# HGRN2/Conformer decoder trunk on one core: where the sums of weight blocks are made, and the order of the first stages

## The chip, the cores and the metric

One core of one Trainium2 chip runs the whole program. The metric is the device time of that core in microseconds (us), the median of three runs. Engines are named as in the profile: PE (TensorE, matmuls), PEld (its weight loads), DVE (VectorE), ACT (ScalarE), POOL (GpSimd), SP (SyncE, which issues nearly all transfers). POOL issues the transfers that add into their destination.

## The reference

Two layers on a sequence of 1024 tokens of width 1024. Each has a token mixer, a squared-ReLU MLP of width 4096, and a layer norm behind each. The first mixer is a gated linear recurrence (8 heads of 128), the second a causal convolution module.

```python
mix = hgrn2_mixer(x, a_w_in[j], lb_all[j], a_norm_g[j], a_w_out[j])      # layer 0
    proj = h @ w_in                       # columns q | forget | value | gate
    f = lb32 + (1.0 - lb32) * sigmoid(fz); k = 1.0 - f
    o = chunkwise_gated_recurrence(silu(q), k, v, cumsum(log f))
    o = rms_norm(o) * norm_g * silu(g);   mix = o @ w_out
mix = conformer_conv_mixer(x, ...)                                        # layer 1
x = layer_norm(DEEPNORM_ALPHA * x + mix, ln_mix_g[i], ln_mix_b[i])
ff = jnp.square(jax.nn.relu(x @ ffn_w1[i])) @ ffn_w2[i]
x = layer_norm(DEEPNORM_ALPHA * x + ff, ln_ffn_g[i], ln_ffn_b[i])
```

## The kernel before

**Products.** Float32 matrices are cut into a high part (a cast to float32r, on ACT) and a low part (the difference, on DVE): `cut` (L412) and `Slots.split` (L70). A product is three matmuls per tile: high by high, high by low, low by high. Many products are also made by a seven-product scheme on 2 by 2 blocks. Its seven forms of the weights run in the order 1, 2, 6, 5, 7, 3, 4 (`ORDER`, L45). With the four blocks w0 to w3 they are: 1: w0; 2: w1; 6: w0+w2+w3; 5: w2+w3; 7: w0+w2; 3: w0+w1+w2+w3; 4: w3. So each group of four blocks needs its sums from somewhere.

**Stages in time.** (a) The values' stage, 0 to 98 us: the value projection in seven forms (`v_products`, L463), 48 matmuls each. (b) The pairs, 109 to about 490 us: twelve pairs of projection blocks (`PAIRS`, L37; a "q" pair makes query and forget gate of one head, a "g" pair the output gates of two heads), seven forms of 12 matmuls each. Between the groups of three matmuls lies a `slot` (L795), four to a form and 28 to a pair. From the second pair on, a slot advances the recurrence of a finished head by 240/308 of a step (`pace`). A recurrence of one head and one half of the tokens has 15 steps (`recurrence`, L603), two can be under way at a time, and the second starts when the first has made seven steps. (c) The output projection. (d) The first MLP up, about 520 to 900 us, in seven forms whose sums are made on DVE (class `Forms`); its results go to DRAM (`hf`). (e) The first MLP down, 900 to 1200 us. (f) The convolution module, to about 1600 us, the second MLP up behind it, and the second MLP down, about 1900 to 2243 us.

**Sums of the values and pairs.** `pair_sums` (L394) makes them in DRAM: two plain transfers on SP copy blocks, then transfers on POOL add the others in, each waiting for the one before it. They are due a number of ticks later (`later`, `tick`; a slot is one tick, a tile of the values' stage four). The sums for pairs 0 to 2 start in the values' stage, those of pair p+3 in pair p. `load_form` (L564) then loads one raw form of 256 KB, and `make_form` (L575) cuts it on ACT and DVE, some forms ahead of its product, into the ring `fs` of six slots. Two of these six lie at 136 and 140 KB, where the last outputs of the values' stage (`VO[4]`) wait for their store.

**Sums of the down MLPs.** Class `Blocks` (L162) makes them anew in both down stages. For forms 1 and 2 it loads two blocks (w0, w2 and w1, w3), adds them on DVE and stores the sum (`pair`). For 6, 5 and 3 it loads two operands and adds, for 7 it loads a stored sum, for 4 a block. Blocks and operands are 512 KB each, and a form of one block is 24 matmuls.

**Orders.** Up to L930 the queues of PE, POOL and SP hold instructions in the order in which they are written. DVE and ACT are ordered by the planner, which sorts by when it expects each input. Behind L930 the planner orders all queues. Each queue runs in order, so an instruction that waits holds all behind it. `spare` (L1227) loads weights of later stages ahead of time during the first MLP: DVE marks the moment, POOL copies a mark into the buffer `next`, SP loads into it. `residual` (L1285) gates the loads of the kept rows `y` in the same way with eight copies on POOL.

Of the kernel before, what the change touches and what calls it, by code (L numbers as in the profile page):

```python
# [8 lines left out]
F32 = mybir.dt.float32  # L9
# [6 lines left out]
P = 128  # L16
# [20 lines left out]
PAIRS = [("q", 0), ("q", 1), ("q", 2), ("g", 0), ("q", 3), ("q", 4), ("g", 1), ("q", 5), ("q", 6), ("g", 2), ("q", 7), ("g", 3)]  # L37
# [122 lines left out]


class Blocks(Slots):  # L162


    def __init__(self, blocks, *rest):
        super().__init__(*rest)
        self.blocks = blocks

    def load(self, pieces=1):

        (i, c), slot = self.todo.pop(0), self.slots()
        self.queue.append(slot)
        w, pair = self.blocks[c]
        srcs = {1: (w[0], w[2]), 2: (w[1], w[3]), 6: (pair[0], w[3]), 5: (w[2], w[3]), 7: (pair[0],), 3: (pair[0], pair[1]), 4: (w[3],)}[i]
        got = [self.raws() for _ in srcs]
        for raw, src in zip(got, srcs):
            self.nc.sync.dma_start(out=raw, in_=src)
        if i in (1, 2):
            self.split(slot, got[0])
            self.vector.tensor_tensor(out=got[1], in0=got[1], in1=got[0], op=ALU.add)  # L180
            self.nc.sync.dma_start(out=pair[i - 1], in_=got[1])
        else:
            if len(got) > 1:
                self.vector.tensor_tensor(out=got[0], in0=got[0], in1=got[1], op=ALU.add)
            self.split(slot, got[0])
        yield
        self.count(slot)
# [78 lines left out]
def body(ctx, tc, d, out):  # L266
# [127 lines left out]
    def pair_sums(t, w, gap, half=False):  # L394
        n = 1 if half else 2

        def flat(x):
            return x.rearrange("a p n -> p a n")

        nc.sync.dma_start(out=flat(t)[:, 0:2], in_=flat(w)[:, 0 : 4 : n] if n == 2 else flat(w)[:, 0:2])  # L400
        if n == 2:
            nc.sync.dma_start(out=flat(t)[:, 2:4], in_=flat(w)[:, 0:2])
        parts = [lambda: nc.gpsimd.dma_start(out=flat(t)[:, 0:2], in_=flat(w)[:, 2:4], accum_op=ALU.add)]
        for i in (2, 3) if n == 2 else (1,):
            parts.append(lambda i=i: nc.gpsimd.dma_start(out=flat(t)[:, i], in_=flat(t)[:, i - 1], accum_op=ALU.add, max_dma_last_dim=4096))
        parts.append(lambda: summed.append(t))
        for i, part in enumerate(parts):
            later((min(i, len(parts) - 2) + 1) * gap, part)

    summed = []  # L410
# [52 lines left out]
    def v_products(i):  # L463
        for t, parts in enumerate(v_form(i)):
            product(banks[:, 4 + t] if i in (2, 5, 3) else banks[:, t], parts, i in (1, 2, 5))
            v_out(i, t)
            if t == 3 and i in (2, 5, 6):
                p = {2: 0, 5: 1, 6: 2}[i]
                pair_sums(psum[p], d["wp"][p], 8)
            tick(4)  # L470

    for k in range(4):
# [17 lines left out]
    psum = [dram.tile([4, P, HT], F32, name=f"psum{p}") for p in range(12)]  # L490
    vsum = dram.tile([2, 2, P, 1024], F32, name="vsum")
    for j in range(2):
        pair_sums(vsum[:, j], d["wv"][:, j], 4, True)
# [9 lines left out]
    cut_x(2, x10)  # L503
    cut_v(2, a1)
    for t in range(NTB):
        v_out(1, t)

# [7 lines left out]

    for k in range(4):
        vector.tensor_tensor(out=x00[:, k], in0=x00[:, k], in1=x01[:, k], op=ALU.subtract)
        cut_x(5, x00, (k,))
    add_v(a2, a2, a3)
    cut_v(5, a2)  # L520
    v_products(2)

    for k in range(4):
        vector.scalar_tensor_tensor(out=t6[:, k], in0=x00[:, k], scalar=-1.0, in1=x11[:, k], op0=ALU.mult, op1=ALU.subtract)
        cut_x(6, t6, (k,))
    add_v(a0, a2, a0)
    cut_v(6, a0)
    outs_v(5)
    sum_v(s7, 0)
    sum_v(a1, 1)  # L530
    v_products(5)

    for k in range(4):
        vector.tensor_tensor(out=x01[:, k], in0=x11[:, k], in1=x01[:, k], op=ALU.subtract)
        cut_x(7, x01, (k,))
    cut_v(7, s7)
    for k in range(4):
        vector.scalar_tensor_tensor(out=x10[:, k], in0=t6[:, k], scalar=-1.0, in1=x10[:, k], op0=ALU.mult, op1=ALU.subtract)
    outs_v(6)
    v_products(6)  # L540

    cut_x(3, x11)
    cut_v(3, a1)
    outs_v(4)
    v_products(7)
    cut_x(4, x10)
# [3 lines left out]
    vector.tensor_tensor(out=sm[:, 0], in0=lg, in1=lg, op=ALU.subtract)  # L550
    nc.scalar.activation(sm[:, 1], sm[:, 0], AF.Exp)
    vector.reciprocal(sm[:, 2], sm[:, 1])
    vector.tensor_tensor(out=sm[:, 3], in0=sm[:, 1], in1=sm[:, 2], op=ALU.mult)
    vector.tensor_tensor(out=lb, in0=sm[:, 3], in1=sm[:, 3], op=ALU.subtract)
    vector.tensor_scalar(out=oml, in0=lb, scalar1=-1.0, scalar2=1.0, op0=ALU.mult, op1=ALU.add)
    vector.tensor_scalar(out=nrm, in0=par[:, NRM : NRM + H], scalar1=1.0 / QSCALE, scalar2=None, op0=ALU.mult)
# [7 lines left out]
    def load_form():  # L564
        n = forms[0]
        if n == 7 * len(PAIRS):
            return
# [1039 lines left out]
```

## Time and profile before

| | |
|---|---|
| runs | 2244.64, 2245.33, 2246.27 us (median 2245.33) |
| profiled execution | 2245.43 us, of which the span is 2243.3 us |
| granted clock, mean | 0.977 |
| busy share of the span | PE 95%, PEld 78%, DVE 68%, ACT 47%, POOL 17% |
| bytes moved | 542.21 MB, mean 242 GB/s |

How to read it. The page gives the busy time of each engine. The view of waits says how long an engine stood still and whose work it then went on with. The timeline lists the instructions of an engine in order of time: start, duration, engine, line, operation, tiles, shapes, count, and in brackets the idle time before it with the releaser. The table of stretches gives for each stretch its length, the busy time of each engine with its count of instructions, then the granted clock as a share of full speed, the share of the time that the 16 DMA engines were busy, and GB/s. The view of transfers gives count, size and the median time from issue to landing. L201 is the line of a helper through which most matmuls and vector instructions go, so the tiles tell them apart: `vw` and `xf` belong to the values' stage, `fs` to the pairs, `qk`, `kd`, `T` and `state` to the recurrences, `fw` to the MLP up, `dw`, `dr` (weights) and `dh` (activations) to the MLP down.

### The profile page before, as it was taken

How to read it: one execution, taken by the hardware profiler on the slowest of the kernel's cores; microseconds unless marked ns; L12 is line 12 of the kernel's file. 1: busy time of each engine (PE TensorE's matmuls, PEld its weight loads, DVE VectorE, ACT ScalarE, POOL GpSimd, SP SyncE). 2: the span in 40 equal slices, each digit the busy share in tenths (PEclk: the TensorE clock that was granted, in tenths of full speed). 3: DMA queues.
4: the chain of work that ended last, by engine and by line, in shares of the span. 5: the costliest groups of instructions: out<-in, count | busy, mean ns of one | idle time of the engine just before them, and what ended most of it. 6: DMA issues, size and time to landing. Idle time of an engine off the chain costs nothing.

```text
span 2243.3 us, 27717 instructions
## 1 busy us (share of the span) xinstructions
PE 2124.4 (95%) x10056; PEld 1749.5 (78%) x10056; DVE 1527.5 (68%) x2078; ACT 1044.3 (47%) x1623; POOL 378.0 (17%) x337
## 2 busy tenths in 40 slices
PE   8799998989999999898999879899999999999998
PEld 6678787868888888677887768688888888877887
DVE  7378676777776666567765779689837444578556
ACT  5345444542365555333444546738662443434333
POOL 1111111001000000100001549549501000000001
PEclk9999999999999999999999989999999999999999
DMA  9866655434358687899997955375455898999762
GB/s 299 233 153 168 173 159 150 126 125 160 114 175 293 235 282 264 328 394 411 374 345 267 363 183 191 115 282 186 160 189 195 294 341 303 398 342 344 240 213 103
DMA packets 191657, 542.21 MB, mean 242 GB/s; under 512 B 18720, under 2 KB 47648, under 8 KB 190496
## 3 DMA queue, kind: packets, MB, share of 16 engines
q1 hardware_dynamic: 185504, 524.71, 64.9%
q0 software_dynamic: 6016, 15.73, 4.4%
q8 instruction: 79, 1.29, 0.2%
q14 instruction: 58, 0.48, 0.1%
HBM read 394.09 MB, written 176.69 MB: 254 GB/s over the span
## 4 chain that ended last, share of the span: by engine, by line
PE 44%; DMA 5%; POOL 3%; DVE 3%; ACT 2%; issue 1%; SPq 0%; DVEq 0%; POOLq 0%; ACTq 0%
PE ps L201 44%; POOL cb L201 3%; DMA next<-in_w_dram 1%; DMA next<-in_wpw_dram 1%; DMA hf<-ht 1%; DMA dr<-in_w_dram 1%; DMA pair<-dr 1%; DVE ps L201 1%; DMA dh<-hf 0%; DVE spare L201 0%; ACT spare L1236 0%; DVE dr L201 0%; ACT prod L1378 0%; ACT dw L70 0%; DMA raw<-in_w_dram 0%
## 5 line engine op out<-in xcount | busy, mean ns | idle before, releaser
L201 PE MATMUL ps<-dw,dh 128*128 128x512 f32 x2688 | 622.8, 394 | 32.2 <-ACT dw L70 20.3
L201 PEld LDWEIGHTS ps<-dw,dh 128*128 128x128 f32 x2688 | 509.9, 190 | 144.2 <-ACT dw L70 22.4
L201 PE MATMUL ps<-x1f,fw 128*128 128x512 f32 x1344 | 308.7, 390 | 0.7 <-DVE fw L201 0.3
L201 PEld LDWEIGHTS ps<-x1f,fw 128*128 128x128 f32 x1344 | 251.2, 188 | 53.0 <-DVE fw L201 0.8
L201 PE MATMUL ps<-xf,fs 128*128 128x512 f32 x1008 | 274.5, 410 | 11.7 <-ACT t L764 11.7
L201 PE MATMUL ps<-xa,wa 128*128 128x512 f32 x1152 | 273.5, 396 | 10.3 <-DMA wa<-ready 9.5
L201 PEld LDWEIGHTS ps<-xa,wa 128*128 128x128 f32 x1152 | 216.9, 190 | 56.4 <-DMA wa<-ready 10.5
L201 POOL TENSOR_TENSOR cb<-cb,prod 128x512 f32<-128x512 f32 x176 | 236.1, 1349 | 35.9 <-ACT prod L1378 25.1
L201 PEld LDWEIGHTS ps<-xf,fs 128*128 128x128 f32 x1008 | 180.6, 192 | 44.4 <-ACT t L764 12.1
L201 DVE SCALAR_TENSOR_TENSOR ps<-u,par,ps 128x512 f32<-128x512 f32 x288 | 204.5, 751 | 13.4 <-ACT ps L1390 9.9
L70 ACT CAST dw<-dr 128x1024 fp32r<-128x1024 f32 x112 | 116.8, 1050 | 183.9 <-DVE dr L201 86.4
L70 ACT CAST dh<-dh 128x1024 fp32r<-128x1024 f32 x112 | 117.1, 1050 | 142.4 <-DMA dh<-hf 139.5
L201 DVE TENSOR_TENSOR dw<-dr,dw 128x1024 fp32r<-128x1024 f32 x112 | 135.9, 1222 | 61.1 <-ACT dw L70 60.6
L201 DVE TENSOR_TENSOR dh<-dh 128x1024 fp32r<-128x1024 f32 x112 | 136.2, 1222 | 57.9 <-ACT dh L70 57.1
L201 PE MATMUL ps<-xc,wa 128*128 128x512 f32 x768 | 174.2, 389 | 0.0
L201 PEld LDWEIGHTS ps<-xc,wa 128*128 128x128 f32 x768 | 144.1, 188 | 29.9
L501 POOL TENSOR_TENSOR mv<-mv,nhalf 128x1 f32<-128x1 f32 x32 | 46.5, 1454 | 713.7 <-DVE mv L201 713.5
L1378 ACT ACTIVATE prod<-u,par 128x512 f32<-128x512 f32 x176 | 126.0, 722 | 61.0 <-POOL cb L201 60.3
L201 DVE TENSOR_TENSOR wa<-raw,wa 128x1024 fp32r<-128x1024 f32 x55 | 71.4, 1299 | 81.7 <-ACT wa L70 81.5
L201 DVE TENSOR_TENSOR dr<-dr 128x1024 f32<-128x1024 f32 x80 | 97.3, 1221 | 40.7 <-DMA dr<-pair 19.8
L70 ACT CAST wa<-raw 128x1024 fp32r<-128x1024 f32 x55 | 57.8, 1050 | 127.8 <-PE ps L201 103.8
L1243 POOL COPY next<-ss 128x1 f32<-128x1 f32 x37 | 20.7, 561 | 538.8 <-DVE ss L1233 234.7
(189 smaller groups left out, 2790.9 us busy)
## 6 DMA issues: line engine op xcount, KB each, us to landing
dr<-in_w_dram SPq DMA_DIRECT2D x128, 512.0 KB, 7.1
wa<-ready SPq DMA_DIRECT2D x122, 512.0 KB, 4.5
dh<-hf SPq DMA_DIRECT2D x112, 512.0 KB, 6.0
ready<-spare SPq DMA_DIRECT2D x74, 512.0 KB, 5.3
dr<-pair SPq DMA_DIRECT2D x64, 512.0 KB, 6.3
raw<-in_w_dram SPq DMA_DIRECT2D x51, 512.0 KB, 4.5
raw<-in_w1q_dram SPq DMA_DIRECT2D x36, 512.0 KB, 4.0
hf<-ht SPq DMA_DIRECT2D x64, 256.0 KB, 5.0
```

The costliest lines, as they stand in the source:

```text
L70: self.nc.scalar.copy(out=slot[:, 0, c], in_=raw[:, c])
L201: return op(*args, **kw)
L501: nc.gpsimd.tensor_tensor(out=dst, in0=src, in1=nhalf[:, :n], op=ALU.pow)
L1243: nc.gpsimd.tensor_copy(out=raw[:, :1], in_=now)
L1378: nc.scalar.activation(tp, u[:, k : k + HT], AF.Copy, scale=tap(j, k))
```

## The change

1. **Pairs.** `pair_sums` for the pairs is gone. The four raw blocks of a pair are loaded (48 loads in place of 84) into five buffers, and `make_form` adds them on DVE: four additions of 128x512 per pair. The ring `fs` has its last two slots at 160 and 164 KB. `PAIRS` has another order. A recurrence that is alone, while others wait or if it is the very first, takes every second step that is given to it.
2. **Values' stage.** DVE and ACT are in written order too, to the end of this stage. Additions and cuts are written between the tiles of the product before the one that uses them, and the forms of the last products are made earlier. The values' own sums stay transfers (`value_sums`).
3. **Second matrices of both MLPs (`w2`).** The class `Blocks` is gone. Sixteen groups of four blocks are summed in DRAM ahead of time by `block_sums`: two plain copies of 1 MiB on SP, then on POOL one adding transfer of 1 MiB and two of 512 KB. Ten are started in the pairs' stage (every eighth form), four in the first MLP up (behind every second group of weights, held back by a transfer of two elements that waits for the last form of that group), two behind the convolution. The down stages load one finished form of 512 KB at a time, with the plain `Slots`.

```diff
-PAIRS = [("q", 0), ("q", 1), ("q", 2), ("g", 0), ("q", 3), ("q", 4), ("g", 1), ("q", 5), ("q", 6), ("g", 2), ("q", 7), ("g", 3)]
+PAIRS = [("q", 0), ("q", 1), ("q", 2), ("q", 3), ("g", 0), ("q", 4), ("q", 5), ("g", 1), ("q", 6), ("q", 7), ("g", 2), ("g", 3)]
-class Blocks(Slots):
...
+    def value_sums(t, w, gap):
...
+        nc.sync.dma_start(out=flat(t), in_=flat(w)[:, 0:2])
+        later(gap, lambda: nc.gpsimd.dma_start(out=flat(t), in_=flat(w)[:, 2:4], accum_op=ALU.add))
+        later(2 * gap, lambda: nc.gpsimd.dma_start(out=flat(t)[:, 1], in_=flat(t)[:, 0], accum_op=ALU.add, max_dma_last_dim=4096))
+    def block_sums(name, layer, c, after=None, gap=0):
+        t = sums[name, layer, c] = dram.tile([4, P, 1024], F32, name=f"sum_{name}{layer}{c}")
+        v, w = t.rearrange("a p n -> p a n"), d[name][layer, c].rearrange("a p n -> p a n")
+        if after is not None:
+            nc.sync.dma_start(out=t[0:4:2, 0, 0:1], in_=after)
+        nc.sync.dma_start(out=v[:, 0:2], in_=w[:, 0:4:2])
+        later(gap // 2, lambda: nc.sync.dma_start(out=v[:, 2:4], in_=w[:, 0:2]))
+        parts = [lambda: nc.gpsimd.dma_start(out=v[:, 0:2], in_=w[:, 2:4], accum_op=ALU.add)]
+        for i in (2, 3):
+            parts.append(lambda i=i: nc.gpsimd.dma_start(out=v[:, i], in_=v[:, i - 1], accum_op=ALU.add, max_dma_last_dim=4096))
         for i, part in enumerate(parts):
-            later((min(i, len(parts) - 2) + 1) * gap, part)
+            later((i + 1) * gap, part)
+    def form(name, layer, c, i):
+        w, t = d[name][layer, c], sums[name, layer, c]
+        return {1: w[0], 2: w[1], 6: t[2], 5: t[1], 7: t[0], 3: t[3], 4: w[3]}[i]
...
+    early_order.enter_context(tc.manual_schedule(engines={mybir.EngineType.DVE, mybir.EngineType.Activation}))
...
-    v_products(2)
+    v_products(2, [lambda: x6(0, 1), lambda: x6(2, 3), lambda: add_v(a0, a2, a0), lambda: cut_v(6, a0)])
     outs_v(5)
     sum_v(s7, 0)
     sum_v(a1, 1)
-    v_products(5)
+    v_products(5, [lambda: x4(0, 1), lambda: x4(2, 3), bounds])
+    outs_v(6)
+    v_products(6, [lambda: x7(0, 1), lambda: x7(2, 3), lambda: cut_v(7, s7)])
+    v_products(7, [lambda: cut_x(3, x11, (0, 1)), lambda: cut_x(3, x11, (2, 3)), lambda: cut_v(3, a1)])
+    outs_v(4)
...
+    def load_block():
+        p, b = divmod(at_block[0], 4)
+        if p < len(PAIRS) and free:
+            at_block[0] += 1
+            raw = blocks_of[p, b] = free.pop(0)
+            nc.sync.dma_start(out=raw, in_=d["wp"][p, b])
     def make_form():
...
+        if i == 6:
+            plus(total, b[0], b[3])
+            plus(b[1], b[1], total)
+        elif i == 5:
+            plus(b[2], b[2], b[3])
+        cut(hi, lo, total if i == 6 else b[{1: 0, 2: 1, 5: 2, 7: 0, 3: 1, 4: 3}[i]])
+        if i == 2:
+            plus(b[0], b[0], b[2])
+        made.append(s)
+        if i in (5, 7, 3, 4):
+            free.append(b[{5: 2, 7: 0, 3: 1, 4: 3}[i]])
+            load_block()
...
+        if len(active) == 1 and (recs or active[0][0] == (0, 0)):
+            alone[0] = not alone[0]
+            if alone[0]:
+                return True
...
     for _ in range(5):
-        load_form()
-    for _ in range(4):
-        make_form()
-    v_products(3)
-    cut_v(4, a3)
-    v_products(4)
-    fs.views += [view(kb, (2, HT), F32R, "fs") for kb in (136, 140)]
+        load_block()
+    v_products(3, [lambda: cut_v(4, a3), make_form, make_form])
+    v_products(4, [make_form])
+    early_order.close()
+    fs.views += [view(kb, (2, HT), F32R, "fs") for kb in (160, 164)]
+    make_form()
...
-            if i == 6 and p + 3 < len(PAIRS):
-                pair_sums(psum[p + 3], d["wp"][p + 3], 12)
+            if (7 * p + ORDER.index(i)) % 8 == 1 and p < len(PAIRS) - 1:
+                block_sums(*to_sum.pop(0), gap=12)
...
-        fw.plan([(i, c) for i in ORDER for c in range(NFC)])
+        fw.plan([form("w2", layer, c, i) for i in ORDER for c in range(NFC)])
...
+        if c in (1, 3, 5, 7):
+            block_sums(*to_sum.pop(0), f[:2, 1, :1].bitcast(F32))
...
-    fw = Blocks(down_weights(0), nc, vector, slots([112, 120, 144, 152, 128, 136, 168], "dw"), raws([192, 196, 200, 204, 160, 164], "dr"), spare, 5, range(12, 56))
+    fw = Slots(nc, vector, slots([112, 120, 144, 152, 128, 136, 168], "dw"), raws([192, 196, 200, 204, 160, 164], "dr"), spare, 5, range(12, 56))
...
+        if half == 1:
+            for of in to_sum:
+                block_sums(*of, mv[:2, 0, 4:5])
```

153 lines of the change are left out of this document (59 added, 94 removed).

## The prediction

> **What bounds the kernel now.** I read the page first, then a table of stretches cut at the stages, then the waits of PE, then the timeline at each long wait.
>
> ```profile
> span 2243.3 us, 27717 instructions
> PE 2124.4 (95%) x10056; PEld 1749.5 (78%) x10056; DVE 1527.5 (68%) x2078; ACT 1044.3 (47%) x1623; POOL 378.0 (17%) x337
> ```
> ```profile
> 0.00:97.70 97.70, 87.55 (x360) 70.74 (x360) 58.59 (x86) 42.01 (x64) 11.86 (x19) 0.97 0.97 282
> 97.70:109.30 11.60, 0.00 (x0) 0.00 (x0) 1.85 (x3) 3.23 (x7) 2.28 (x4) 0.71 0.57 143
> 109.30:480.00 370.70, 345.79 (x2129) 287.93 (x2130) 272.05 (x552) 172.12 (x405) 43.65 (x42) 0.97 0.54 148
> ...
> 520.00:900.00 380.00, 379.35 (x1729) 314.25 (x1728) 262.94 (x329) 186.45 (x275) 16.24 (x21) 1.00 0.62 216
> 900.00:1200.00 300.00, 274.30 (x1169) 223.47 (x1168) 197.67 (x202) 121.16 (x124) 21.58 (x24) 0.95 0.94 360
> ...
> 1900.00:2243.00 343.00, 329.58 (x1443) 271.74 (x1441) 220.89 (x220) 129.76 (x142) 10.46 (x8) 0.98 0.75 276
> ```
>
> PE is the bound: it stands still for 2243.3 - 2124.4 = 119 us in all, and the change leaves its matmuls alone. So it can win only idle PE time, and the slow clock behind it. In the stretches that it touches, idle PE time is 10 us in the values' stage, 12 at its end, 25 in the pairs, 26 in the first MLP down and 13 in the last. In two of them the transfers are near their limit: 97% and 94% of the engines' time. The first MLP up has PE busy throughout; there the change can only lose.
>
> ```profile
> PE ps L201 <- ACT dw L70: 20.3, 5, 8.8
> PE ps L201 <- DVE qk L201: 17.7, 10, 4.4
> PE ps L201 <- ACT t L764: 11.7, 1, 11.7
> PE ps L201 <- ACT dh L70: 10.2, 1, 10.2
> ```
>
> Total, count and longest of each wait. These four are half of the 119 us, and all lie where the change works.
>
> **Part 1, values' stage in written order: -2 us.**
>
> ```profile
> 35.70 31.17 PE L201 MATMUL ps<-vw,xf 128*128 128x512 f32 x125 [4.25 <-DVE vw L201]
> ```
> ```profile
> 64.91 2.00 ACT L413 CAST vw<-vr 128x1024 fp32r<-128x1024 f32 x2 [7.01 <-DMA vr<-vsum]
> ```
>
> PE waits 4.25 us for the second half of form 5's weights, because the planner put later forms' work on DVE first. Written order removes that wait. But forms 7 and 3 use sums that come by transfer, and ACT is found waiting 7.01 us for one of them. With everything 4 us earlier PE meets these late transfers, even if the pairs' sums no longer crowd them. I take half; the ends are -4.3 and, if a written queue stands behind a late load, +7.
>
> **Part 2, hand-over to the pairs: -13 us.**
>
> ```profile
> 108.18 0.62 ACT L413 CAST fs<-pr 128x512 fp32r<-128x512 f32 x1 [5.55 <-DMA vd<-vo]
> ```
> ```profile
> 109.33 19.57 PE L201 MATMUL ps<-xf,fs 128*128 128x512 f32 x78 [11.65 <-ACT t L764]
> ```
>
> After two forms PE waits for a copy of its own result, and that copy stands in ACT's queue behind casts into the ring slots under `VO[4]`, whose stores are late. The new slots at 160 and 164 KB have no such neighbour, and the first casts are written between the tiles of forms 3 and 4. The raw blocks need form 7's stores to land first, but two forms of 48 matmuls lie between. The whole wait goes, with the slow clock behind it (1.7 us, next part). Ends: -13.4 and 0, if the block loads turn out as late as the stores did.
>
> **Part 3, order of pairs and pace: -18 us.**
>
> ```profile
> 262.06 1.23 PE L201 MATMUL ps<-qk 128*128 128x128 f32 x8 [4.28 <-DVE qk L201]
> 263.08 1.92 PE L201 MATMUL ps<-kd 128*128 128x128 f32 x8
> 264.65 1.63 PE L201 MATMUL ps<-xf,fs 128*128 128x512 f32 x3
> ...
> 282.15 0.94 PE L201 MATMUL ps<-xf,fs 128*128 128x512 f32 x3
> 282.93 1.05 PE L201 MATMUL ps<-qk 128*128 128x128 f32 x8
> 283.82 1.06 PE L201 MATMUL ps<-kd 128*128 128x128 f32 x8
> ...
> 361.54 1.67 PE L201 MATMUL ps<-qk 128*128 128x128 f32 x8 [3.76 <-DVE qk L201]
> ...
> 458.92 2.04 PE L201 MATMUL ps<-qk 128*128 128x128 f32 x8 [5.42 <-ACT wb L70]
> ```
>
> Counting the pace through by hand (28 slots to a pair, 240/308 of a step each, 15 steps to a recurrence), heads 3, 5 and 7 start one to two slots after their own pair has ended, since the stock of recurrences had run low or out. DVE has then only just been given the gates, and PE stands before the first `qk` product. These are the three rows above, the third with a cast as its named releaser. In the new order the same count finds heads 3, 5 and 7 starting 1.1, 0.9 and 0.6 pairs after theirs, so DVE's chain is done by then. That is 4.28 + 3.76 + 5.42 = 13.5 us. The three groups behind the first wait take 4.78 us where the same three take 3.05 at full clock, so each long wait costs 1.7 us more: 18.6 in all. Ends -18.7 and -9.
>
> **Part 4, the additions on DVE: +8 us.**
>
> ```profile
> L201 DVE TENSOR_TENSOR fs<-pr,fs 128x512 fp32r<-128x512 f32 x84 | 57.7, 688 | 48.7 <-ACT fs L413 43.3 <-DMA pr<-in_wp_dram 4.4 <-DMA u<-od 0.8
> ```
>
> Four additions for each of 12 pairs, the size of this row's: 48 x 0.688 = 33 us. DVE goes from 272 to 305 of 370.7 us (73% to 82%), its free time from 99 to 66 us. PE's smaller `qk` waits are 17.7 - 4.4 - 4.28 - 3.76 = 5.3 us; by the free time they would grow by half, 2.6 us. The additions also lie inside a form's own chain, so I take 8; ends 0 and +33.
>
> **Part 5, the new sums in the pairs and in the first MLP up: +8 us.**
>
> ```profile
> q0 software_dynamic: 6016, 15.73, 4.4%
> ```
> ```profile
> psum<-in_wp_dram POOLq DMA_DIRECT2D x12, 512.0 KB, 8.0
> ...
> vsum<-in_wv_dram POOLq DMA_DIRECT2D x2, 1024.0 KB, 11.1
> ```
>
> Adding transfers moved 15.73 MB in 4.4% of 2243 us, 159 GB/s with all engines; plain ones reach 360 (the fifth stretch). A group of `w2` takes 2.1 MB of each: 13.2 + 5.8 = 19 us of the engines. Ten make 190 us in the pairs, where the old sums fall away (half the size: 9.5 us for each of nine) and 36 raw loads of 256 KB (26 us): the share goes from 0.54 to about 0.75, below the 0.94 at which the MLP waits. POOL had as many transfers per pair before. I take +2 there (0 to +10). In the first MLP up four groups add 76 us, 0.62 to 0.82; the first product with late weights would cost PE directly, and I take +6 (0 to +68, first rival).
>
> **Part 6, first MLP down: -19.5 us.**
>
> ```profile
> dr<-in_w_dram SPq DMA_DIRECT2D x128, 512.0 KB, 7.1
> ...
> dr<-pair SPq DMA_DIRECT2D x64, 512.0 KB, 6.3
> ...
> pair<-dr SPq DMA_DIRECT2D x32, 512.0 KB, 6.9
> ```
> ```profile
> 999.52 7.45 PE L201 MATMUL ps<-dw,dh 128*128 128x512 f32 x24 [2.81 <-ACT dw L70]
> 1015.79 13.45 PE L201 MATMUL ps<-dw,dh 128*128 128x512 f32 x48 [8.82 <-ACT dw L70]
> ```
> ```profile
> L1289 POOL COPY y<-dw x8: 181/182/10272, 901.7 to 912.6; 128x1 f32<-128x1 f32 x8
> ```
>
> (128 + 64 + 32) / 16 = 14 transfers of 512 KB for a group become 7. Over eight groups that is 29 MB, 27% of what the stretch moves at 360 GB/s, so the share falls from 0.94 to about 0.69. The waits of 2.81 and 8.82 us for a weight form then go (-11). At the start PE waits 10.2 us for `dh`. There one tiny copy on POOL took 10.27 us where the median is 0.18, and SP stood behind it; DVE was busy without a gap. With DVE's additions gone from there I take half (-5). The slow clock of two waits adds -3.5. Ends: -25, and +12 if the last group's adding transfers stand on POOL ahead of these copies.
>
> By the Trainium skill ("SBUF — State Buffer", section "Who interferes with whom") a DVE instruction with two SBUF inputs shuts out a GpSimd instruction that reads SBUF, for its whole length. The trace agrees: 10.27 against 0.18 us. That speaks against part 4, which puts 48 such instructions beside POOL's; the last rival.
>
> **Part 7, second MLP down: -7 us.**
>
> ```profile
> 2020.01 8.60 PE L201 MATMUL ps<-dw,dh 128*128 128x512 f32 x28 [5.17 <-ACT dw L70]
> ```
>
> The same halving of transfers takes this wait and its clock, 6.9 us; ends -7 and 0. DVE's 80 additions leave as well, hidden behind PE either way. Against it, one more recurrence step is left over behind the pairs (8 of the last head's 15 remain in place of 7): +1.
>
> **Sum:** -2 - 13 - 18 + 8 + 8 - 19.5 - 7 + 1 = -42.5. From the profiled execution, 2245.43 us (median 2245.33), that makes 2203.
>
> **The rivals.**
>
> *POOL's queue holds SP (slower).* In the MLP up the planner orders POOL's queue. If a group's three adding transfers stand one behind the other with a `next` copy last, that copy waits 11.1 + 8.0 + 8.0 = 27 us, and SP's loads of weights behind it. For it:
>
> ```profile
> SPq L1244 <- POOL next L1243: 21.0, 13, 6.2
> ```
>
> SP already waits up to 6.2 us for such copies. Against it: the planner queues a transfer when it believes its input there. Weights are cut three forms ahead, 3 x 24 matmuls x 379.35/1729 us = 15.8, so PE would lose 11.3 us for a group, up to 17 at longer landings. At 14 for each of four, without part 5's +6, and with the start of the MLP down at +11 in place of -5: 2203 - 6 + 56 + 16 = 2269. It decides the sign from 12 us for a group.
>
> *DVE becomes the bound of the pairs.* All 33 us of additions reach PE: 2203 + 25 = 2228. For it: DVE already releases PE's waits there. Against: it has 99 us free.
>
> *Fewer transfers don't shorten the MLP down.* Its waits are latency, stores of `hf` and their reload, or the loads of `spare`, which stay. Without parts 6 and 7: 2203 + 26.5 = 2230. For it: the start waits on `dh`, not on weights.
>
> *POOL is shut out in the pairs.*
>
> ```profile
> L501 POOL TENSOR_TENSOR ss<-ss,nhalf 128x4 f32<-128x4 f32 x16 | 20.3, 1268 | 254.9 <-DVE ss L201 254.9
> ```
>
> Each of 16 recurrences needs this POOL instruction, with two empty steps behind it (2 x 1.1 / 0.78 = 2.8 us, a slot being 370.7/336 us). Were each held for half of 10.27 us, PE would lose 2.3 x 16 = 37: 2240. So far the mean is 1.27 us, little above one instruction. By the page named above, this is what a denser DVE would do.
>
> **How the numbers follow.** Chances: the forecast 0.50, with its own range 2180 to 2222; DVE as bound 0.13; no gain in the MLP down 0.13; POOL shut out 0.06; POOL holding SP 0.18. About 0.2% (4.5 us) can be told from no change, so faster ends at 2240.8. The first three cases and part of the fourth are faster: 0.78; same 0.05; slower 0.17. The range 2180 to 2256 leaves out the better ends of parts 3 to 6 together (0.05) and most of the slower rival (0.14).
>
> **What would show it.** Right: no wait of over 5 us between the last `vw` and first `fs` products; no wait of about 4 us before a first `qk` product except head 0's; the share of transfers in the MLP down near 0.7 and no `dw` wait over 3 us; PE busy over 375 of 380 us in the MLP up. Wrong: waits on `fw` in the MLP up with SP standing behind POOL; many waits on `qk`, `state` or `o` in the pairs with DVE over 85%; a longer wait for `dh` at the start of the MLP down.

## The result, and the profile after

The kernel after takes 2168.78 us (median of four runs, 2167.55 to 2170.50) against 2245.56 us (2244.64 to 2246.27) on the same chip: a ratio of 0.9659, with a 95% interval from 0.9642 to 0.9676. It is faster by 76.8 us, where 42.5 were forecast, and lies 11 us below the range.

The head of the page after, and its row of the adding transfers (packets, MB, share of the 16 engines' time):

```profile
span 2165.8 us, 27376 instructions
...
PE 2103.7 (97%) x10056; PEld 1739.1 (80%) x10056; DVE 1452.7 (67%) x2046; ACT 1043.8 (48%) x1623; POOL 388.8 (18%) x349
...
q0 software_dynamic: 9792, 36.70, 9.5%
```

PE runs the same 10056 matmuls. It stands still for 2165.8 - 2103.7 = 62 us where it had stood for 119, and the matmuls themselves take 20.7 us less, at a mean granted clock of 0.992 in place of 0.977.

To see where, both traces are cut at the same products of PE, by their operands: the first and the last `xf,fs`, the first `dw,dh`, the convolution's first `xa,wa`, its first `wa,xa` (the middle), and the first `xc,wa` (the second half of the second MLP up). Stretches of the kernel after (columns as before: busy time of each engine, granted clock, DMA share, GB/s):

```profile
0.00:98.40 98.40, 82.13 (x337) 65.56 (x338) 64.39 (x92) 44.02 (x67) 5.98 (x14) 0.97 0.68 215
98.40:479.60 381.20, 356.51 (x2220) 296.99 (x2218) 301.99 (x611) 182.40 (x429) 54.36 (x45) 0.98 0.70 189
479.60:900.80 421.20, 413.56 (x1872) 341.14 (x1871) 280.85 (x361) 200.25 (x307) 27.93 (x33) 0.99 0.72 240
900.80:1214.40 313.60, 310.18 (x1378) 256.65 (x1377) 196.11 (x224) 146.27 (x160) 29.47 (x47) 0.99 0.93 337
1214.40:1375.90 161.50, 161.50 (x754) 134.12 (x752) 141.93 (x214) 113.51 (x186) 134.28 (x107) 1.00 0.59 212
1375.90:1679.10 303.20, 300.86 (x1396) 248.41 (x1393) 220.69 (x307) 161.84 (x249) 125.49 (x96) 1.00 0.64 220
1679.10:2165.80 486.70, 478.95 (x2114) 396.25 (x2112) 246.72 (x240) 195.47 (x230) 11.32 (x8) 0.99 0.67 236
```

The same stretches of the kernel before, those that moved most:

```profile
92.10:490.50 398.40, 359.92 (x2216) 298.99 (x2215) 282.30 (x568) 183.04 (x432) 47.31 (x46) 0.97 0.56 152
...
902.50:1253.00 350.50, 319.63 (x1377) 260.37 (x1375) 231.09 (x251) 136.73 (x143) 31.90 (x40) 0.96 0.92 353
1253.00:1446.00 193.00, 170.08 (x754) 138.03 (x753) 151.72 (x217) 122.49 (x197) 137.59 (x112) 0.93 0.58 211
```

| stretch, us | before | after | difference |
|---|---|---|---|
| values' stage | 92.1 | 98.4 | +6.3 |
| hand-over and pairs | 398.4 | 381.2 | -17.2 |
| output projection, MLP up 1 | 412.0 | 421.2 | +9.2 |
| MLP down 1 | 350.5 | 313.6 | -36.9 |
| convolution, first half | 193.0 | 161.5 | -31.5 |
| its second half, start of MLP up 2 | 302.1 | 303.2 | +1.1 |
| the rest | 495.2 | 486.7 | -8.5 |

Two rows carry the result: the first MLP down, and the convolution behind it, which the prediction doesn't name. In the convolution (here its first half) PE now has no idle time at all (161.50 busy of 161.50). Before, it had stood there for 23 us and run at a clock of 0.93.

### The profile page after: what moved, and what is told of

It is laid out like the page before. It is cut to its first block, busy times and chain, and to the rows that moved or that the text cites. A ratio compares the mean times of both kernels' runs of the same rounds, so it can differ in the third digit from the quotient of the medians.

```text
span 2165.8 us, 27376 instructions
## 1 busy us (share of the span) xinstructions
PE 2103.7 (97%) x10056; PEld 1739.1 (80%) x10056; DVE 1452.7 (67%) x2046; ACT 1043.8 (48%) x1623; POOL 388.8 (18%) x349
## 3 DMA queue, kind: packets, MB, share of 16 engines
q0 software_dynamic: 9792, 36.70, 9.5%
## 4 chain that ended last, share of the span: by engine, by line
PE 76%; DMA 10%; DVE 7%; POOL 3%; ACT 2%; issue 2%; SPq 0%; DVEq 0%; POOLq 0%; ACTq 0%
PE ps L173 76%; POOL cb L173 3%; DMA u<-od 2%; DVE qk L173 1%; DMA wa<-ready 1%; DMA dh<-hf 1%; DMA next<-in_wpw_dram 1%; DMA hf<-ht 1%; DMA y<-kept 1%; DMA hf<-hr 1%; DMA vr<-in_wv_dram 1%; DVE fs L173 0%; DVE fw L173 0%; DVE xr L173 0%; ACT xf L399 0%
## 5 line engine op out<-in xcount | busy, mean ns | idle before, releaser
L173 PE MATMUL ps<-dw,dh 128*128 128x512 f32 x2688 | 612.9, 390 | 3.4 <-ACT dh L70 3.4
L173 PE MATMUL ps<-xa,wa 128*128 128x512 f32 x1152 | 268.8, 392 | 0.0
L173 DVE SCALAR_TENSOR_TENSOR ps<-u,par,ps 128x512 f32<-128x512 f32 x288 | 198.6, 748 | 9.8 <-ACT ps L1402 8.5
L173 PE MATMUL ps<-vw,xf 128*128 128x512 f32 x336 | 82.3, 406 | 16.3 <-ACT vw L399 11.3
```

The costliest lines, as they stand in the source:

```text
L173: return op(*args, **kw)
```

## The experiments

### Where the two large gains come from

**The new sums of `w2` taken back, and made alone.** The first run is the kernel after with part 3 of the change undone; the second is the kernel before with part 3 alone.

```diff
-    fw = Slots(nc, vector, slots([112, 120, 144, 152, 128, 136, 168], "dw"), ...)
+    fw = Blocks(down_weights(0), nc, vector, slots([112, 120, 144, 152, 128, 136, 168], "dw"), ...)
...
-                block_sums(*to_sum.pop(0), gap=12)
```

> The changed kernel with part 3 undone: the w2 sums are made in the down stages as before (class Blocks), no sums ahead of time. If all of the gain in the first MLP down (36.9 us) and in the first half of the convolution (31.5 us) comes from part 3, both go, and 8.5 us of the last stage; the 9.2 us that the stretch of output projection and MLP up lost come back: 2169 + 77 - 9 = 2237 us. If the convolution gained by another cause (the earlier stages, or the planner's order behind them), only 2169 + 45 - 9 = 2205 us.

> The kernel before with part 3 alone; both sets of sums then go over POOL's queue in the pairs' stage. Part 3 as the cause of both gains: 2245 - 77 + 9 = 2177 us, plus up to 15 us for the crowded pairs, 2177 to 2192. Part 3 as the cause of the MLP down alone: 2209 to 2224 us.

The first took 2219.88 us (ratio 0.9891, 0.9877 to 0.9906), the second 2224.35 (0.9898, 0.9870 to 0.9926). Stretches of the first (pairs, MLP down, convolution), then of the second:

```profile
100.80:467.40 366.60, 350.80 (x2220) 291.60 (x2218) 302.53 (x612) 182.15 (x429) 28.54 (x15) 1.00 0.26 84
...
878.80:1232.30 353.50, 320.61 (x1378) 261.63 (x1376) 233.01 (x253) 138.35 (x146) 32.04 (x40) 0.95 0.92 351
1232.30:1422.80 190.50, 168.72 (x755) 137.15 (x753) 152.45 (x218) 122.56 (x197) 137.80 (x112) 0.94 0.58 216
```
```profile
96.30:535.90 439.60, 372.75 (x2216) 307.14 (x2215) 281.78 (x567) 181.41 (x430) 78.19 (x76) 0.93 0.86 231
...
957.20:1275.00 317.80, 311.62 (x1378) 257.41 (x1377) 198.52 (x227) 148.36 (x163) 30.72 (x47) 0.99 0.92 332
1275.00:1436.50 161.50, 161.50 (x754) 134.12 (x752) 141.93 (x214) 113.49 (x186) 134.36 (x107) 1.00 0.57 213
```

Without part 3 the MLP down takes 353.5 us and the convolution 190.5, as before; with it alone they take 317.8 and 161.5, as after. So part 3 makes both gains, and nothing else is needed for them. The medians miss the first figures expected, 2237 and 2177 to 2192, because of the pairs. Without the new sums the pairs take 366.6 us, 14.6 less than in the kernel after. With the pairs' own sums by transfer beside the new ones the transfer engines are busy for 0.86 of the time, and the pairs lose 41 us against before. That eats most of the gain further on: alone, part 3 makes the kernel 1% faster (20 us by the medians); taken out of the kernel after, it costs 51 us by the medians. The pairs' new loads, which clear their transfers, and part 3 belong together.

**Transfers or additions.** Part 3 takes two things out of the down stages: seven transfers of 512 KB for each group, and DVE's additions. Each was put back alone into the kernel after.

```diff
+        got = [self.raws() for _ in range(2 if i in (1, 2, 6, 5, 3) else 1)]
+        self.nc.sync.dma_start(out=got[0], in_=src)
+        if len(got) > 1:
+            self.nc.sync.dma_start(out=got[1], in_=w[2] if i == 1 else w[3])
+        self.split(slot, got[0])
+        if i in (1, 2):
+            self.nc.sync.dma_start(out=pair[i - 1], in_=got[1])
```
```diff
+        if i in (6, 5, 3):
+            self.vector.tensor_tensor(out=raw, in0=raw, in1=raw, op=ALU.max)
...
+        if i in (1, 2):
+            self.vector.tensor_tensor(out=raw, in0=raw, in1=raw, op=ALU.max)
```

> The changed kernel, with the transfers of before put back in both down stages (a second load for forms 1, 2, 6, 5 and 3, a store for 1 and 2, none of them used) and no addition on DVE. Theory of transfers: the load on the transfer engines delays the weights and the chain that loads the next stage's weights ahead, so 55 to 77 us come back: 2224 to 2246. Theory of DVE: the additions were what held that chain (DVE shuts POOL out): 2169 to 2180 us.

> The changed kernel, with one more 128x1024 instruction on DVE (the maximum of a form with itself) for forms 1, 2, 6, 5 and 3 in both down stages, 80 in all, and no added transfer. Theory of transfers: 2169 to 2176 us. Theory of DVE: 2215 to 2246 us. Both in part: between, 2180 to 2215.

With the transfers 2260.31 us, with the additions 2169.68 (one run each). Stretches of the MLP down, first with the transfers, then with the additions:

```profile
903.30:1263.80 360.50, 318.04 (x1377) 260.20 (x1375) 196.00 (x219) 144.22 (x149) 21.71 (x42) 0.94 0.96 357
```
```profile
903.20:1213.70 310.50, 309.20 (x1377) 255.30 (x1377) 237.78 (x263) 146.81 (x159) 42.01 (x47) 1.00 0.93 337
```

The transfers alone bring everything back, the convolution too (192.3 us). They overshoot the 2246 expected by 14 us: the MLP down is 10 us longer than in the kernel before, and why wasn't settled. The additions cost nothing: DVE has 42 us more to do (237.78 against 196.11), and PE doesn't notice.

**Bytes, or the places that they take.** The old transfers also take buffers of the raw ring and stand in SP's order. Here the same number runs from DRAM to DRAM, into memory that nobody reads.

```diff
+        for k in range({1: 2, 2: 2, 6: 1, 5: 1, 3: 1}.get(i, 0)):
+            self.nc.sync.dma_start(out=pair[{1: 0, 2: 2, 6: 4, 5: 5, 3: 6}[i] + k], in_=w[k])
```

> The kernel after, with seven more transfers of 512 KB for each group of w2 in both MLP downs, as many as the kernel before had more, but from DRAM to DRAM, which take no room of the raw ring and nothing waits for. If the bytes alone made the waits (transfer engines full), the first MLP down takes 345 to 365 us, the convolution 185 to 193 us, the kernel 2235 to 2262. If it was the ring of six raw blocks and the order on SP's queue that held the weights up, 313 to 320 us and 161 to 166 us, the kernel 2168 to 2185.

The run took 2334.95 us and says nothing on the question. Nothing held the copies back, so all 112 ran at the start of the program: the values' stage took 262.5 us with the transfer engines busy for 0.94 of it, the MLP down 317.0. A second kernel holds each group of copies behind a tiny store of a weight block made two forms earlier.

```diff
+            self.nc.sync.dma_start(out=pair[a : a + n, 0, 0:1], in_=self.recent[-3][:n, 1, :1].bitcast(F32))
+            for k in range(n):
+                self.nc.sync.dma_start(out=pair[a + k], in_=w[k])
```

> As the run with DRAM to DRAM copies in the MLP downs, but each group of copies stands behind a tiny store of the weight block made two forms earlier, so that they run where the transfers of the kernel before ran. They take no room of the raw ring. If the bytes alone held the weights up, the first MLP down takes 340 to 365 us, the convolution 180 to 195 us, the kernel 2215 to 2262. If it was the ring of six raw blocks and SP's order, 313 to 322 us and 161 to 166 us, the kernel 2168 to 2185.

```profile
903.30:1256.10 352.80, 320.75 (x1378) 261.28 (x1376) 192.92 (x216) 140.18 (x146) 21.50 (x41) 0.96 0.95 361
1256.10:1448.10 192.00, 168.91 (x753) 137.29 (x753) 152.55 (x217) 122.45 (x197) 137.73 (x112) 0.94 0.59 212
```

2246.31 us (one run; one of the kernel before beside it took 2241.07), and both stretches are within 2.3 us of those of the kernel before. The bytes alone are enough; the ring isn't needed to explain it, and the small stores are not what held SP's queue (its waits there for a `dw` make 2.4 us in the MLP down). The copies themselves do stand in SP's queue ahead of later loads, so it isn't shown that they would cost as much from another queue.

**How bytes in the MLP down reach the convolution.** The kernel loads the convolution's weights ahead of time: `spare` fetches 37 pieces one after the other through the buffer `next`, cuts them and stores them in DRAM as `ready`. It begins them in the MLP up and goes on through the MLP down. First the POOL marks of `next` before (columns: count, shortest/median/longest ns, first and last start), then PE's wait in the convolution before, then the marks after:

```profile
L1243 POOL COPY next<-ss x37: 183/184/2014, 660.5 to 1283.7; 128x1 f32<-128x1 f32 x37
```
```profile
1305.14 8.59 PE L201 MATMUL ps<-xa,wa 128*128 128x512 f32 x24 [9.48 <-DMA wa<-ready]
```
```profile
L1253 POOL COPY next<-ss x37: 178/185/2309, 652.4 to 1193.7; 128x1 f32<-128x1 f32 x37
```

Before, the last piece was marked at 1283.7, 31 us into the convolution, and PE waited 9.48 us for a `ready` weight soon after. After, it came at 1193.7, 21 us ahead of it, and no wait is left. (The wait for `ready` is only the largest of the 22.9 us of idle time there; the others were for results of ACT and DVE.) If that is the link, the kernel before must gain as much from these loads alone, with its transfers and additions left as they are:

```diff
-... raws(run(160, 2, 4), "sum"), spare, 3, range(44))
+... raws(run(160, 2, 4), "sum"), spare, 5, range(44))
```

> The kernel before, with the loads of the convolution's first weights into spare room started sooner (five items for each form instead of three in the MLP up). Theory: the convolution was long because these loads, which come in between the transfers of the MLP down, ended late: it shrinks from 193 to about 165 us, and the kernel takes 2214 to 2224. Rival: what the convolution lacked was transfer room at the end of the MLP down itself, whatever was loaded before: the convolution stays at 188 to 193 us, the kernel at 2240 to 2250.

```profile
903.40:1236.10 332.70, 315.53 (x1378) 258.83 (x1377) 228.56 (x252) 137.18 (x148) 27.46 (x37) 0.97 0.93 353
1236.10:1397.70 161.60, 161.60 (x754) 134.05 (x752) 140.29 (x213) 116.54 (x190) 134.27 (x107) 1.00 0.60 212
```
```profile
L1243 POOL COPY next<-ss x37: 181/185/2252, 655.7 to 1199.8; 128x1 f32<-128x1 f32 x37
```

One digit changed in the kernel before (pieces for each eight forms of weights), and it takes 2195.66 us, 53 less than the median beside it (one run). The convolution stands at 161.6 us with no wait. The MLP down gives 17.8 us as well; it moves 117.59 MB in place of 123.78, at the same 353 GB/s. The first MLP up pays nothing (411.3 us) at a share of 0.70 in place of 0.62. More was gained than the theory had forecast, for it had left the MLP down out.

The other way round, the kernel after with these loads begun later:

```diff
-... raws(run(160, 2, 4), "sum"), spare, 3, range(44))
+... raws(run(160, 2, 4), "sum"), spare, 3, range(16, 44))
...
-... raws([192, 196, 200, 204, 160, 164], "dr"), spare, 5, range(12, 56))
+... raws([192, 196, 200, 204, 160, 164], "dr"), spare, 6, range(12, 56))
```

> The kernel after with the loads of the convolution's weights started later (none for the first 16 forms of the MLP up) and made somewhat denser in the MLP down (six items for each eight forms instead of five). If the convolution's wait is set by when these loads end, they end 20 to 60 us later, the convolution takes 165 to 193 us and the kernel 2173 to 2205. If the room that the fewer transfers of w2 leave is enough whenever they start, the convolution stays at 161 to 164 us, the kernel at 2166 to 2174.

2186.27 us, in the band of the first theory, but for another reason in the main. The last mark came only 24 us later (1218.0), still ahead of the convolution, which lost 4.5 us. The first MLP up lost 8.1 (429.3 us), and why it did isn't settled. This run doesn't decide whether late loads would undo the kernel after in full.

All sixteen kernels of this document, cut at the same products, bear the link out. In four of them the last mark came 28 to 31 us into the convolution: the kernel before, the one without the new sums, the one with the transfers put back and the one with the gated copies. There the convolution takes 190.5 to 193.0 us, and PE waits 9.1 to 10.1 us for a `ready` weight. In the other twelve the last mark came 8 to 36 us ahead of it and no wait for `ready` is left: it takes 161.5 or 161.6 us, and 166.0 in the run with late loads, where the mark came closest. How late loads delay ACT and DVE there too wasn't traced.

### The pairs

**Order and pace.** The kernel after with the old `PAIRS` and without the half pace of a lone recurrence:

```diff
-PAIRS = [("q", 0), ("q", 1), ("q", 2), ("q", 3), ("g", 0), ...
+PAIRS = [("q", 0), ("q", 1), ("q", 2), ("g", 0), ("q", 3), ...
...
-        if len(active) == 1 and (recs or active[0][0] == (0, 0)):
...
```

> The kernel after with the order of the pairs and the pace of the kernel before. Theory (the three long first qk waits came from the order, part 3): they come back, 13.5 us and 5 us of slow clock, the pairs take 395 to 402 us and the kernel 2183 to 2190. Rival (the order is worth little; the transfers of raw blocks in place of the sums' or the hand-over did it): 2166 to 2174.

2195.38 us (ratio 0.9764, 0.9748 to 0.9780), 5 us beyond the theory's band. In the profiled execution (2202.19 us) the pairs take 404.5 us, 23.3 more than after and 2.5 beyond the band; the MLP down is 7.3 us longer too, and no run tells why. Its timeline of PE, the long waits before a first `qk` product:

```profile
259.15 2.05 PE L173 MATMUL ps<-qk 128*128 128x128 f32 x8 [4.63 <-DVE qk L173]
...
361.63 1.41 PE L173 MATMUL ps<-qk 128*128 128x128 f32 x8 [3.75 <-DVE qk L173]
...
467.61 2.05 PE L173 MATMUL ps<-qk 128*128 128x128 f32 x8 [5.42 <-DVE qk L173]
```

The three restarts are back: 13.8 us against the 13.46 of the three rows that the prediction shows. The longest wait for `qk` of the kernel after, 3.5 us, stands before the very first `qk` product. The last of the three now names DVE's `qk`, which fits the reading of the third row. Order and pace were taken back together, so the share of each isn't known.

**DVE's additions doubled.** Behind each addition of the pairs' blocks stands an idle one of the same size:

```diff
             vector.tensor_tensor(out=out, in0=x, in1=y, op=ALU.add)
+            vector.tensor_tensor(out=out, in0=out, in1=out, op=ALU.max)
```

> The kernel after with an idle second instruction (max of a block with itself, same size) behind each of the 44 additions of the pairs' blocks, so DVE has 30 us more in the pairs. If DVE is no bound, 2168 to 2173; if each addition costs as the prediction had it (8 of 33 us), 2175 to 2180; if DVE is the bound of the pairs (the rival), 2195 to 2203.

2179.71 us (ratio 0.9702, 0.9682 to 0.9722), by the ratios 9.7 us above the kernel after. In the profiled execution (2177.30 us) DVE is busy 24.2 us longer in the pairs (326.20 against 301.99), and the stretch takes 387.2 us, 6.0 more. A quarter of DVE's added time reaches PE there, so DVE is no bound at 84%.

**What the new sums cost there.** The pairs of the run without them stand above: 0.26 for the share of the transfers, 366.6 us, a clock of 1.00. PE is idle there for 15.8 us, in the kernel after for 24.7; the other 5.7 of the 14.6 us are matmuls at a clock of 0.98. The wait of DVE for `u` in the pairs, and the transfers of `u` there (count, size, median us to landing), first of the run without the sums, then of the kernel after:

```profile
DVE u L201 <- DMA u<-od: 8.5, 7, 2.4
```
```profile
u<-od SPq DMA_DIRECT2D x12, 256.0 KB, 3.1
```
```profile
DVE u L173 <- DMA u<-od: 15.7, 6, 5.1
```
```profile
u<-od SPq DMA_DIRECT2D x12, 256.0 KB, 7.6
```

`od` is a recurrence's output, which goes to DRAM and comes back as `u` for the gates' product. Beside the big sums its way back takes 7.6 us in place of 3.1, and DVE's queue stands for it 7 us longer. PE's waits grow as well, for what DVE makes next, in the same order:

```profile
PE ps L201 <- DVE qk L201: 13.1, 13, 3.5
...
PE ps L201 <- DVE state L201: 0.8, 2, 0.4
```
```profile
PE ps L173 <- DVE qk L173: 16.6, 11, 3.5
PE ps L173 <- DVE state L173: 6.2, 5, 2.5
```

Cut at the very ends of the stretch the first two are 12.9 and 0.8, so these two waits grow by 9.1 us, and they account for the 8.9 us of idle time. That they come by way of `u` is argued from the two traces and not shown: other small transfers landed later too, and no run took that one out.

### The values' stage

PE's timeline there, after:

```profile
30.97 2.97 PE L173 MATMUL ps<-vw,xf 128*128 128x512 f32 x12 [1.49 <-DVE vo L173]
35.44 3.01 PE L173 MATMUL ps<-vw,xf 128*128 128x512 f32 x12 [1.49 <-DVE vo L173]
39.99 16.76 PE L173 MATMUL ps<-vw,xf 128*128 128x512 f32 x72 [1.55 <-DVE vo L173]
62.91 0.80 PE L173 MATMUL ps<-vw,xf 128*128 128x512 f32 x1 [6.15 <-ACT vw L399]
```

and DVE's, where each cut of a slice waits for its cast on ACT:

```profile
46.98 0.69 DVE L173 SCALAR_TENSOR_TENSOR xr<-xr 128x512 f32<-128x512 f32 x1
48.35 0.69 DVE L173 TENSOR_TENSOR xf<-xr,xf 128x512 fp32r<-128x512 f32 x1 [0.69 <-ACT xf L399]
```

The old wait of 4.25 us is gone, but written order puts a subtraction, its cast and its cut one behind the other for each slice, and form 4's slices ahead of form 7's, though form 4 comes last. Form 7 then waits 6.15 us for its weights, whose cast on ACT stands behind those slices. Two runs: the planner's order again, and another written order, with the subtractions of a block together and form 7 ahead of form 4.

```diff
-    early_order.enter_context(tc.manual_schedule(engines={mybir.EngineType.DVE, mybir.EngineType.Activation}))
```
```diff
-        for k in ks:
-            diff(x01, x11, x01, (k,))
-            cut_x(7, x01, (k,))
+        diff(x01, x11, x01, ks)
+        cut_x(7, x01, ks)
...
-    v_products(5, [lambda: x4(0, 1), lambda: x4(2, 3), bounds])
+    v_products(5, [lambda: x7(0, 1), lambda: x7(2, 3), lambda: x4(0, 1), lambda: x4(2, 3)])
```

> The kernel after with the values' stage ordered on VectorE and ScalarE by the planner instead of as written; everything else stays. Before, the planner's order cost 92.1 us for the stage and 11.65 us at the hand-over; after, the written order took 98.4 us and no hand-over. If the written order by itself made the stage longer, the stage shrinks to 92 to 95 us; if it also was what removed the hand-over, a wait of 5 to 12 us between the last vw and the first fs product comes back (in the table, in the pairs), and the kernel takes 2168 to 2178. If the new slots alone removed the hand-over, it takes 2161 to 2165.

> The kernel after with three changes in the written order of the values' stage: VectorE's subtractions of form 5's x run one slice ahead of the casts they are cut from, all four subtractions of a block stand together instead of one by one between casts, and form 7's x stands ahead of form 4's, which is needed last. Theory (VectorE and ScalarE wait for each other slice by slice, and form 4's early work makes form 7 late): the waits of 3 x 1.5 us in form 5 and of 6.15 us before form 7 shrink, the values' stage takes 87 to 93 us, the kernel 2157 to 2164. Rival (the stage waits on the vector work as such, or on late loads): 96 to 99 us, 2166 to 2171.

With the planner's order 2168.48 us (2163.99 to 2171.55), with the other written order 2165.84 (2164.61 to 2169.12); neither can be told from the kernel after (ratios 0.9654, 0.9625 to 0.9683, and 0.9645, 0.9613 to 0.9678). The stage itself did shrink, to 92.9 and 90.3 us, as the theory had it, but the kernel's times that were expected with it (2161 to 2165, 2157 to 2164) were not reached. PE in the run with the planner's order, from the last values' forms to the pairs' first:

```profile
62.78 30.26 PE L173 MATMUL ps<-vw,xf 128*128 128x512 f32 x132 [0.81 <-ACT vo L438]
92.88 7.42 PE L173 MATMUL ps<-xf,fs 128*128 128x512 f32 x32
```

There is no wait between them, so it isn't the written order that removed the hand-over; the new slots and the forms made earlier, which this run keeps, do it without. The two runs gave 3 to 4.5 us back in the pairs, and 2.7 and 2 to 3 in the MLP down and behind the convolution. Why a head start of 5 to 8 us doesn't last wasn't settled.

### A better version

The first MLP up had lost 9.2 us to four groups of sums; behind the convolution the transfers had room (0.64). One run moves five groups there, another joins this with the new order of the values' stage.

```diff
-        if c in (1, 3, 5, 7):
-            block_sums(*to_sum.pop(0), f[:2, 1, :1].bitcast(F32))
...
+            if layer == 1 and half == 0 and c in (0, 1, 2, 4, 6) and j == 0:
+                block_sums(*to_sum.pop(0), w1[:2, 1, :1].bitcast(F32), 2)
```

> The kernel after with the four groups of w2's sums that ran in the first MLP up, and one more, moved behind the convolution, into the first half of the second MLP up (0.64 of the transfer engines' time is used there, and PE waits only 2 us). Theory: the first MLP up goes back to 411 to 413 us, the stage behind the convolution grows by 0 to 4 us, the kernel takes 2158 to 2166. Rival (the transfers are only as dear there): that stage grows by 8 to 15 us, and the kernel takes 2167 to 2176.

> Both: the sums moved and the values' stage reordered. If both theories hold and the gains add, 2147 to 2158; if neither, 2166 to 2176.

The move alone took 2166.45 us (0.9649, 0.9621 to 0.9676), no different from the kernel after. The MLP up went back to 413.3 us, but the stretch behind the convolution grew to 313.7, by 10.5, as the rival had it: five groups cost as much there at a share of 0.81. Both together took 2154.92 us (2150.96 to 2161.65; ratio 0.9598, 0.9567 to 0.9630), faster than both kernels, by 14 us against the kernel after. Its first two stretches:

```profile
0.00:87.70 87.70, 80.73 (x337) 64.35 (x338) 63.73 (x92) 43.88 (x67) 5.98 (x14) 1.00 0.77 242
87.70:468.60 380.90, 355.25 (x2219) 295.62 (x2218) 302.58 (x611) 182.02 (x429) 53.87 (x45) 0.98 0.72 189
```

Here the values' gain lasts (87.7 us, and pairs no longer than after). The two give more together than each alone; no run tells why.

## Why the prediction was wrong

The sign was right, and the long waits that the prediction said would go did go. The size was wrong, above all in one step. That the total is not further off is luck: the stretches beat the sum by 35 us, where this step alone was short by 49, and parts 1 and 5 failed the other way.

**Part 6 failed, by 49 us.** It took 19.5 us from the waits of the first MLP down and stopped there. Two things were missing.

The first is the convolution (-31.5 us), which stands in no term of the sum. The wait of 9.48 us for `ready` weights was in the trace before, as was the clock of 0.93 there. The prediction followed the transfers that part 3 removes up to the end of the stage that they run in, not to the loads for the next stage that run between them. The runs show the link: the bytes back alone, 192.0 us; the loads of `next` ahead of time alone, 161.6.

The second is the MLP down itself, -36.9 in place of -19.5. PE's waits in the whole stretch, before and after:

```profile
PE ps L201 <- ACT dw L70: 15.1, 4, 8.8
PE ps L201 <- ACT dh L70: 10.2, 1, 10.2
PE ps L201 <- DVE xa L201: 4.4, 1, 4.4
```
```profile
PE ps L173 <- ACT dh L70: 3.4, 1, 3.4
```

The waits named (2.81, 8.82 and the start) account for most of the old idle time, and only one is left, 3.4 us for `dh`. But the stretch had 30.9 us of idle PE time (350.50 - 319.63) and 9.5 us of slower matmuls (319.63 - 310.18), where the prediction took 26 from its table cut at 900 and 1200 and counted half of the start. Ending the cut at 1200 left out the stage's last 53 us, with the 4.4 us for `xa`, and the next stage's trouble.

The share of the transfers, forecast at 0.69, stayed at 0.93. All transfers of the stage before, then after (packets, bytes, mean rate):

```profile
DMA packets 35454, 123.78 MB, mean 353 GB/s; under 512 B 3861, under 2 KB 5141, under 8 KB 35436
```
```profile
DMA packets 30776, 105.79 MB, mean 337 GB/s; under 512 B 3328, under 2 KB 4864, under 8 KB 30757
```

18 MB fewer, not 29. The issues of `dr` and `pair` in the stage fall from 96 to 48 (25 MB), while more `ready` and `next` pieces now fit in (72 in place of 64). The stage is 11% shorter, and a full set of engines moves less: 353 / 0.92 = 384 GB/s before, 337 / 0.93 = 362 after. So the share doesn't tell whether PE waits: at 0.92 it stood for 30.9 us, at 0.93 for 3.4. What did change is how soon the next operands land: `dh` after 4.8 us (median) in place of 6.7, the loads of `dr` after 5.7 and 6.6 in place of 7.4 and 8.3.

**Part 5 was too small in the pairs:** +2 forecast, beyond its upper end of +10 measured, 14.6 by the run without the sums. The share was forecast well (0.75; it is 0.70). What failed is the reading that nothing waits below 0.94: at 0.70 the small transfer `u`, on a chain of dependent steps, landed after 7.6 us in place of 3.1, and PE stood 8.9 us longer (the link between the two is argued). That the pairs as a whole came within 3 us of the sum is luck: parts 2 to 4 gave some 10 us more than forecast there. In the first MLP up +6 was forecast, +9.2 measured.

**Part 1 had the wrong sign:** -2 forecast, +6.3 measured in the stage, near its upper end of +7, but by slice-by-slice waits between DVE and ACT, not by a late load. The wait of 4.25 us did go with the written order; with the planner's order it is back (4.25 again).

**Parts 2, 3, 4 and 7 held in their mechanism.** Hand-over: no wait is left (-13 forecast, 11.65 us and its clock gone). All 1008 of the pairs' projection matmuls together waited 0.0 us after:

```profile
L173 PE MATMUL ps<-xf,fs 128*128 128x512 f32 x1008 | 275.5, 411 | 0.0
```

Order and pace of the pairs: -18 forecast, -23.3 by the run with the old ones, beyond the better end of -18.7. Additions: +8 forecast; 6.0 us for 44 more of them makes 6.5 for 48, and up to 11 by the ratios, if a second set costs what the first does. Second MLP down: -7 forecast, -8.5 measured in the last stretch. Parts 2 to 4 with the leftover step make -22; the run without the new sums shows 366.6 - 398.4 = -31.8, and some 4 us of this are in none of the single runs.

**The rivals.** POOL's queue holding SP: fallen. The MLP up lost 9 us where 56 were priced, and at the start of the MLP down the eight copies, priced at +11, take less in all (longest 2.3 us where it was 10.3, median longer):

```profile
L1301 POOL COPY y<-dw x8: 178/1260/2316, 902.4 to 911.4; 128x1 f32<-128x1 f32 x8
```

This rival's threshold was also worked out wrong: with its own +16 at the start of the MLP down, the sign would have turned from 8 us for a group (2203 - 6 + 16 + 4 x 8 = 2245), not from 12. DVE as the bound of the pairs: fallen, by the doubled additions. No gain in the MLP down: fallen. POOL shut out in the pairs: its price didn't come, and what there is of it isn't clearly the additions' doing. Its instruction for the recurrences, after:

```profile
L487 POOL TENSOR_TENSOR ss<-ss,nhalf x16: 1027/1401/4953, 154.5 to 498.2; 128x4 f32<-128x4 f32 x16
```

One of the sixteen took 4.95 us, where the longest before took 1.57; the median stayed (1.40 against 1.39). With DVE's additions doubled it is the same, 4.95 and 1.40, and the kernel before with the new sums alone, without these additions, has one of 3.42. The rule of the Trainium skill ("SBUF — State Buffer", "Who interferes with whom") that the prediction weighed here isn't refuted, but 96 additions in place of none gave it no price that shows.

## What to carry to other kernels

Where transfers are near their limit, list every transfer that runs in the stage, those for later stages too, and ask which of them gets earlier when some leave: the gain may lie in the next stage, and a preload started earlier may win it without the rest of the change (here 53 us for one digit, where the whole change won 77). Price a large background transfer by the small ones on the path that it may lengthen, not by the share of the engines alone. Cut the table of stretches where the stages begin and end, so that no stage's tail falls between two rows.

## What the hardware showed that was not expected

The same set of transfer engines at the same share (0.92 and 0.93) moved 384 GB/s worth of full time in one kernel and 362 in the other, so a share can't be turned into bytes by one rate. Adding transfers were cheaper than estimated: 36.70 MB in 9.5% of 2165.8 us are 178 GB/s, where the trace before gave 159. And bytes that nobody waits for, from DRAM to DRAM on SP's queue, held PE up as much as the loads that they stood for: 352.8 and 192.0 us for the MLP down and the convolution, 350.5 and 193.0 in the kernel before.
